# Weight sums on another engine, gate and sums in PSUM, and other PSUM banks for the early parts, in a one-layer encoder kernel on one core

## The chip, the cores and the metric

The kernel runs on one core of a Trainium2 chip. The metric is the device time of one execution in microseconds (us); the median of three runs stands for a kernel. The engines of the core are TensorE (PE in the profile; PEld is its weight load), VectorE (DVE), ScalarE (ACT), GpSimd (POOL) and SyncE (SP), which starts the DMA transfers.

## The reference

One layer of a streaming encoder on a sequence of 1024 tokens of 1024 features, in float32:

```
x = LN1(alpha*x + 0.5*SwiGLU_1(x))                      # FFN 1, width 2816
x = LN2(alpha*x + W_o[ RMS(FoX(x)) || RMS(ShortConv(x)) ])  # mixer
x = LN3(alpha*x + 0.5*SwiGLU_2(x))                      # FFN 2, width 2816
x = LN4(alpha*x + sigmoid(x W_g + b_g) * (p[i] W_p))      # gated embedding

def _swiglu(x, w_in, w_out):
    gu = x @ w_in
    gate, up = jnp.split(gu, 2, axis=-1)
    return (jax.nn.silu(gate) * up) @ w_out
```

FoX is causal attention with 8 heads of 64 and a forget gate; ShortConv is a gated causal convolution of width 3 over 512 channels. Both read one input projection.

## The kernel before, in words

**Products.** Every float32 operand is split into a high part (a cast by ScalarE) and a low part (source minus high part, by VectorE); `put` does this (line 122, its subtraction is line 124). `mm3` (140) then makes three matmuls of 128x512 (lines 142 to 144): high by high, high by low, low by high. The two large matrix products of each FFN and the mixer's input products go by a scheme with seven block products in place of eight (that of Strassen and Winograd), which needs sums of blocks of the activations (S1 to S4) and of the weights.

**Input products.** `turn0` (173) splits the blocks A11 and A12 of the activations. `turn1` (178) makes, for each of four slices k, the sums S3, S1, S2, S4 and the copy A22, and splits them. Its sums run through `tt` (135, operation at 137): a11 and a12 on GpSimd, s3, s1, s2 and s4 on VectorE, into SBUF tiles. In FFN 1 the blocks come from DRAM (`get_dram`, 198), elsewhere from r, the tokens by features, by TensorE transposes and a ScalarE pass (`get_ln`, 203). So that TensorE has work while the sums are made, the two of the seven products that need A11 and A12 alone run first for some column blocks: "early parts" (`ahead`, 279, with `part1`, 245, which evacuates the second product by VectorE at line 250). FFN 1 and FFN 2 have 10 early parts (`ffn_in`, 300; one step of `turn1` from the second part on in FFN 1), the mixer has 8 (loop at line 630; a step of `turn1` behind parts 4 to 7). All products take their bank from the one pool of eight PSUM banks. The rest runs in `pair` (284) and `part2` (260, evacuations at 262), with weight sums on GpSimd (`combos`, 253).

**Output products.** `ffn_out` (380) runs the seven products n = 0 to 6 one after the other. A product has 11 steps j of 12 matmuls; in each, a block H of the hidden activations and a block w of weights are split. The weight blocks come from functions `w_b11` to `w_b22` (406 to 430); `w_t3`, `w_t2` (417), `w_t4` and `w_t1` make 11 sums each on GpSimd, so 44 in each FFN. After a product, VectorE adds half of its four banks to r (line 467). r begins as the residual: `rest` (513) loads a quarter of x after another, and a multiplication follows, by ScalarE in FFN 1 (`init1`, line 523) and by GpSimd in FFN 2 (`init2`, line 976); this is spread over the products n = 0 to 3. In n = 5 and 6 the tokens are normalised (`norm`, 215; the power at 223 on GpSimd).

**Gate.** After FFN 2, `affine` (1051) applies the gain and offset of the third norm to r on GpSimd (lines 1055, 1056), rows 0 to 3 as soon as they are normalised. The product with W_g needs eight weight blocks (`w_block`) in each half. `gate` (1023) adds the bias on VectorE (1028) into an SBUF tile, takes the sigmoid on ScalarE (1029), multiplies by the embedding on GpSimd (1030) and adds to r on VectorE (1031). `finish_out` (1038) makes the last norm, four operations of VectorE for each row tile (1047, 1048), and stores.

The order of each engine's instructions is set by a scheduler that simulates the program, except where the code asks for program order. Each engine runs its list in order, and a DMA queue too.

Of the kernel before, what the change touches and what calls it, by code (L numbers as in the profile page):

```python
# [25 lines left out]
H = 8  # L26
# [25 lines left out]
def kernel(ctx: ExitStack, tc: tile.TileContext, x, xT, pT, f1_in, f1_out, f2_in,  # L52
# [60 lines left out]

    def load(src):
# [63 lines left out]
    def turn1(get, new=temp):  # L178
# [36 lines left out]
    def norm(r):  # L215
        st = small.tile([P, 2, 6], F32, name="st", tag="st")
        for i in range(2):
            nc.vector.bn_stats(st[:, i, :], r[:, half(i)])
        mv = small.tile([P, 2], F32, name="mv", tag="mv")
        nc.vector.bn_aggr(mv, st)  # L220
        rs = small.tile([P, 1], F32, name="rs", tag="rs")
        nc.vector.tensor_scalar(rs, mv[:, 1:2], LN_EPS, None, op0=add)
        nc.gpsimd.tensor_tensor(rs, rs, mhalf[:, 0:1], op=ALU.pow)
        nc.vector.tensor_scalar(r, r, mv[:, 0:1], rs, op0=sub, op1=mult)

# [74 lines left out]
    def ffn_in(w_in, get, early, wait, free, first=None):  # L300
# [60 lines left out]
        t1 = turn1(get, lambda: silp.tile([P, HB], F32, name="tt", tag="sil"))  # L361
# [6 lines left out]
        drain(t1)  # L368
        free()
# [8 lines left out]
        up.release()  # L378

    def ffn_out(w_out, init, after0, after1, extra=None):  # L380
# [24 lines left out]

        def w_b11(j):
# [12 lines left out]

        def w_t4(j):  # L420
            return tt(nc.gpsimd, load(w_out[j + NP][:, half(0)]), ztile(NP + j), sub)

        def w_t1(j):
            return tt(nc.gpsimd, load(w_out[j][:, half(1)]), ztile(j), sub)
# [14 lines left out]
        for n, (_, get_w, b, (i, nn)) in enumerate(prods):  # L439
# [21 lines left out]
            for t in range(4):  # L461
                for j, h, w in late:
                    mm3(ps[t], (h[0][:, tok(t)], h[1][:, tok(t)]), w, False, j == NP - 1, onto)
                if extra is not None and n in (0, 4):
                    mm(ps[t], ones_k, extra[n // 4], start=False, stop=True, skip_group_check=True)
                rs = r[4 * i + t][:, half(nn)]
                nc.vector.scalar_tensor_tensor(rs, ps[t], 0.5, rs, op0=mult, op1=add)
                if n == 6:
                    norm(r[4 + t])
# [159 lines left out]
    t1 = turn1(get_ln(r, 0), lambda: up.tile([P, HB], F32, name="tt", tag="u"))  # L629
    for i in range(8):  # L630
# [340 lines left out]
    def init2(r):  # L971
# [3 lines left out]
        for o, n in rest(r, z_d[1]):  # L975
            tc.keep_in_program_order(nc.gpsimd.tensor_tensor(o, o, gains[n], op=mult))
            yield

    def row_pair(o, n):


        a = [temp() for _ in range(n + 1)]
        for i, t in enumerate(a):
            nc.vector.memset(t[0:33], 0.0)
            for q in (0, 32):
                nc.sync.dma_start(t[q:q + 1], rows[3:4, half(i)])
        if n:
            nc.vector.tensor_tensor(a[1][0:33], a[1][0:33], a[0][0:33], op=sub)
        t, l = a[n], temp()
        nc.vector.tensor_scalar(t[0:33], t[0:33], 2 * ALPHA, None, op0=mult)  # L990
# [5 lines left out]
    def after0(r):  # L996
# [6 lines left out]
                        [row_pair(extra[n], n) for n in range(2)])  # L1003
# [19 lines left out]
    def gate(hf, t, ps, c0, w=HB, eng=nc.gpsimd):  # L1023
# [14 lines left out]
    def finish_out(t):  # L1038
# [5 lines left out]
        stt = nc.vector.scalar_tensor_tensor  # L1044
# [37 lines left out]
    for n in (1, 0):  # L1082
        for t in range(4):
            for q in range(2 if (n, t) == (0, 3) else 1):
# [5 lines left out]
                gate(1, t, ps, n * HB + q * w, w, nc.vector if w < HB else nc.gpsimd)  # L1090
# [3 lines left out]
    for t in outs:  # L1094
        finish_out(t)
# [72 lines left out]
```

## Time and profile before

| | before |
|---|---|
| runs, us | 1951.53, 1953.48, 1954.69 |
| median, us | 1953.48 |
| the profiled execution, us | 1955.81 |
| its span in the profile, us | 1954.0 |
| TensorE busy, us | 1874.5 |
| VectorE busy, us | 1442.4 |
| GpSimd busy, us | 997.6 |
| ScalarE busy, us | 799.8 |

The span runs from the first to the last instruction of the profile; 1.8 us lie outside it. The stages follow each other: input products of FFN 1 to about 445 us, its output products to 659, the mixer's input to 915, attention to 1140, the mixer's output to 1180, the input products of FFN 2 to 1596, its output products to 1844, then the gate. Busy shares of an engine do not say who waits for whom; a stretch is read by the matmuls in it, the granted clock (PEclk, 1.00 is 2.4 GHz) and what ended TensorE's waits.

### The profile page before, as it was taken

The page shows a single profiled execution, that of the slowest core. Times are in us where ns is not written, and L with a number is a line of the kernel's source. Part 1 is how long each engine was busy: PE and PEld are TensorE (multiplying, and loading weights), DVE is VectorE, ACT ScalarE, POOL GpSimd, SP SyncE. Part 2 cuts the span into 40 slices and gives each one's busy share as a digit, 9 for nine tenths or more (in the row PEclk, how much of TensorE's full clock was granted, in tenths as well). Part 3 has the DMA queues.
Part 4 walks back from the last instruction along what each step waited for, and adds up shares of the span by engine and source line. Part 5 has one row for each costly group of instructions (what it writes and reads, how often), then busy time and mean ns, then how long its engine had stood idle before and what let it go on. Part 6 is the DMA issues. An engine that isn't in the chain of part 4 may idle for free.

```text
span 1954.0 us, 25776 instructions
## 1 busy us (share of the span) xinstructions
PE 1874.5 (96%) x8632; PEld 1540.8 (79%) x8632; DVE 1442.4 (74%) x1999; ACT 799.8 (41%) x1420; POOL 997.6 (51%) x725
## 2 busy tenths in 40 slices
PE   8799999999999989999899999999999999899896
PEld 7688888888788868887688778888888887688685
DVE  7966555548767689976988877976555568987968
ACT  5322333325444553444665526433333334344430
POOL 2787566545550154431841322697565546850673
PEclk9899999999999999999999999999999999999998
DMA  7454323239555533378963123455332249554312
GB/s 238 150 185 163 117 102 119 96 121 379 171 186 178 183 115 119 105 253 273 267 172 91 56 91 118 146 194 178 105 124 93 97 139 365 186 189 152 123 59 98
DMA packets 167938, 307.60 MB, mean 157 GB/s; under 512 B 18503, under 2 KB 26951, under 8 KB 167805
## 3 DMA queue, kind: packets, MB, share of 16 engines
q1 hardware_dynamic: 167804, 305.95, 46.4%
q8 instruction: 68, 1.11, 0.2%
q14 instruction: 66, 0.53, 0.1%
HBM read 221.93 MB, written 83.95 MB: 157 GB/s over the span
## 4 chain that ended last, share of the span: by engine, by line
PE 76%; DVE 12%; issue 5%; DMA 3%; POOL 2%; ACT 1%; SPq 0%; DVEq 0%; ACTq 0%; POOLq 0%
PE ps L143 23%; PE ps L144 22%; PE ps L142 22%; DVE wl L124 4%; DVE tt L137 1%; PE pt L830 1%; PE pt L142 1%; PE pt L143 1%; PE pt L144 1%; PE ps_s L785 1%; PE po L838 1%; PE ps_s L782 1%; DVE S L124 1%; DVE pr L792 1%; PE po L837 1%
## 5 line engine op out<-in xcount | busy, mean ns | idle before, releaser
L142 PE MATMUL ps<-S,wh 128*128 128x512 f32 x896 | 350.8, 392 | 14.0 <-ACT S L123 6.5
L143 PE MATMUL ps<-S,wh 128*128 128x512 f32 x896 | 350.8, 392 | 4.0 <-DVE S L124 4.0
L144 PE MATMUL ps<-S,wl 128*128 128x512 f32 x896 | 350.2, 391 | 0.4 <-DVE wl L124 0.4
L123 ACT CAST wh<-tmp 128x512 fp32r<-128x512 f32 x268 | 164.7, 621 | 355.7 <-PE ps L143 268.5
L124 DVE TENSOR_TENSOR wl<-tmp,wh 128x512 fp32r<-128x512 f32 x268 | 256.8, 959 | 32.4 <-ACT wh L123 32.2
L143 PE MATMUL ps<-wl,wh 128*128 128x512 f32 x616 | 243.3, 395 | 15.1 <-DVE wl L124 15.1
L124 DVE TENSOR_TENSOR wl<-raw,wh 128x512 fp32r<-128x512 f32 x231 | 200.1, 870 | 75.7 <-ACT wh L123 75.4
L123 ACT CAST wh<-raw 128x512 fp32r<-128x512 f32 x239 | 146.6, 621 | 261.7 <-PE ps L143 208.3
L137 POOL TENSOR_TENSOR tmp<-raw 128x512 f32<-128x512 f32 x112 | 159.9, 1428 | 165.2 <-DVE wl L124 106.0
L144 PE MATMUL ps<-wh,wl 128*128 128x512 f32 x616 | 241.1, 391 | 0.0
L142 PE MATMUL ps<-wh 128*128 128x512 f32 x616 | 226.4, 393 | 0.7 <-ACT wh L123 0.7
L137 POOL TENSOR_TENSOR tmp<-raw,tmp 128x512 f32<-128x512 f32 x112 | 158.0, 1411 | 114.4 <-DVE wl L124 54.3
L142 PEld LDWEIGHTS ps<-S,wh 128*128 128x128 f32 x896 | 169.1, 189 | 50.5 <-ACT S L123 7.3
L143 PEld LDWEIGHTS ps<-S,wh 128*128 128x128 f32 x896 | 169.2, 189 | 40.5 <-DVE S L124 5.7
L144 PEld LDWEIGHTS ps<-S,wl 128*128 128x128 f32 x896 | 169.2, 189 | 36.2 <-DVE wl L124 1.1
L343 POOL TENSOR_TENSOR c<-c,sil 128x512 f32<-128x512 f32 x78 | 124.0, 1591 | 74.2 <-DVE c L250 43.3
L143 PEld LDWEIGHTS ps<-wl,wh 128*128 128x128 f32 x616 | 116.2, 189 | 45.8 <-DVE wl L124 22.2
L124 DVE TENSOR_TENSOR wl<-H,wh 128x512 fp32r<-128x512 f32 x154 | 147.4, 957 | 2.3 <-ACT wh L123 2.2
L142 PEld LDWEIGHTS ps<-wh 128*128 128x128 f32 x616 | 115.5, 188 | 25.8 <-ACT wh L123 1.8
L144 PEld LDWEIGHTS ps<-wh,wl 128*128 128x128 f32 x616 | 116.3, 189 | 23.5
L137 POOL TENSOR_TENSOR c<-c 128x512 f32<-128x512 f32 x88 | 128.1, 1460 | 6.7 <-DMA c<-e_d 1.9
L262 DVE TENSOR_TENSOR u<-ps,u 128x512 f32<-128x512 f32 x136 | 92.0, 683 | 47.2 <-PE ps L144 47.1
(299 smaller groups left out, 3988.0 us busy)
## 6 DMA issues: line engine op xcount, KB each, us to landing
raw<-in_f_in SPq DMA_DIRECT2D x216, 256.0 KB
h_d<-c SPq DMA_DIRECT2D x154, 256.0 KB
H<-h_d SPq DMA_DIRECT2D x154, 256.0 KB
raw<-in_f_out SPq DMA_DIRECT2D x132, 256.0 KB
z_d<-r SPq DMA_DIRECT2D x16, 512.0 KB
raw<-in_w_conv_in SPq DMA_DIRECT2D x32, 256.0 KB
r<-z_d SPq DMA_DIRECT2D x32, 256.0 KB
s_d<-s SPq DMA_DIRECT2D x28, 256.0 KB
```

The source lines that it names most:

```text
L123: nc.scalar.copy(h, src)
L124: (eng or nc.vector).tensor_tensor(l, src, h.bitcast(F32), op=sub)
L137: eng.tensor_tensor(t, a, b, op=op)
L142: mm(ps, a[0], b[0], start=first, stop=False, skip_group_check=onto)
L143: mm(ps, a[0], b[1], start=False, stop=False, skip_group_check=onto)
L144: mm(ps, a[1], b[0], start=False, stop=last, skip_group_check=onto)
L262: nc.vector.tensor_tensor(o, ps, u, op=add)
L343: nc.gpsimd.tensor_tensor(c, c, sil.pop((j, i, hf)), op=mult)
L782: mm(st[:, b:b + n], q["QA"][:, tok(t)], q["KA"][:, b:b + n], start=True, stop=False)
L785: mm(st[:, b:b + n], q["QB"][:, tok(t)], q["KB"][:, b:b + n], start=False, stop=True)
L792: nc.vector.tensor_scalar(pr[:, 0:w], pr[:, 0:w], l, None, op0=mult)
L830: nc.tensor.transpose(pv[:, j, t, :], prs[t][:, tok(2 * jp + j)], ident)
```

## The change

The four weight sums of each output step go from GpSimd to VectorE (`w_t3`, `w_t2`, `w_t4`, `w_t1`), three of them held back until a certain split of the product before (`sums`). The first product's evacuation goes to ScalarE as a scaled copy, and the residual is loaded and added during products 1 to 4. In `turn1` VectorE's sums are written to PSUM tiles of a pool of their own (three banks, while the early products have five), in FFN 2 and the mixer the A22 source too; in the mixer a step of `turn1` comes behind parts 1 to 4. In the gate the bias is added by a matmul, and sigmoid, product and sum read PSUM; the last norm's scale and shift go to ScalarE, its gain to VectorE and its offset to GpSimd (VectorE for the last row). GpSimd's `affine(0)` starts after the last of the eight powers.

```diff
+    def banks_anew(*n):
+        for q in reversed(psb):
+            q.release()
+        psb[:] = [pool(f"psb{i}", m, space=PSUM) for i, m in enumerate(n)]
...
-            s3 = tt(nc.vector, a11, a21, sub, new)
+            s3 = tt(nc.vector, a11, a21, sub, tbank)
...
-            a22 = get(1, k + 4, new)
+            a22 = get(1, k + 4, got or new)
...
-            s1 = tt(nc.vector, a21, a22, add, new)
+            s1 = tt(nc.vector, a21, a22, add, tbank)
...
-            s2 = tt(nc.vector, s1, a11, sub, new)
+            s2 = tt(nc.vector, s1, a11, sub, tbank)
...
-            s4 = tt(nc.vector, a12, s2, sub, new)
+            s4 = tt(nc.vector, a12, s2, sub, tbank)
...
-        t1 = turn1(get, lambda: silp.tile([P, HB], F32, name="tt", tag="sil"))
+        banks_anew(5, 3)
+        t1 = turn1(get, lambda: silp.tile([P, HB], F32, name="tt", tag="sil"),
+                   None if get is get_dram else tbank)
...
         drain(t1)
+        banks_anew(8)
...
+        def sums(n, j, o, a, b, op):
+
+            with tc.issue_after(done[n - 1, min(j + 5, NP - 1)]):
+                nc.vector.tensor_tensor(o, a, b, op=op)
+            return o
...
-            return tt(nc.gpsimd, b22, b12, sub, lambda: ztile(NP + j))
+            return tt(nc.vector, b22, b12, sub, lambda: ztile(NP + j))
...
-            tc.keep_in_program_order(nc.gpsimd.tensor_tensor(t, t, ztile(j), op=add))
-            return t
+            return sums(2, j, t, t, ztile(j), add)
...
-            return tt(nc.gpsimd, load(w_out[j + NP][:, half(0)]), ztile(NP + j), sub)
+            return sums(3, j, temp(), load(w_out[j + NP][:, half(0)]), ztile(NP + j), sub)
...
-                if n < 4 and j in (1, 3, 5, 7):
+                if n > 0 and n < 5 and j in (1, 3, 5, 7):
                     next(late_init)
...
-                nc.vector.scalar_tensor_tensor(rs, ps[t], 0.5, rs, op0=mult, op1=add)
+                if n == 0:
+                    nc.scalar.activation(rs, ps[t], AF.Copy, scale=0.5)
+                else:
+                    nc.vector.scalar_tensor_tensor(rs, ps[t], 0.5, rs, op0=mult, op1=add)
...
-        for i, nn in ((1, 0), (0, 1), (0, 0), (1, 1)):
+        for i, nn in ((0, 1), (0, 0), (1, 1), (1, 0)):
...
-        for o, _ in rest(r, x):
-            nc.scalar.mul(o, o, ALPHA)
+        for z, o, _ in rest(r, x):
+            if z is o:
+                nc.scalar.mul(o, o, ALPHA)
+            else:
+                nc.vector.scalar_tensor_tensor(o, z, ALPHA, o, op0=mult, op1=add)
...
-        if i > 3:
+        if 0 < i < 0 + 5:
             next(t1)
+    banks_anew(8)
...
-        pl, c = load(ple_d[tok(row), cs]), temp((P, w))
-        nc.vector.tensor_tensor(c, ps, bg[:, cs], op=add)
-        nc.scalar.activation(c, c, AF.Sigmoid)
-        eng.tensor_tensor(c, c, pl, op=mult)
-        nc.vector.tensor_tensor(r[row][:, cs], r[row][:, cs], c, op=add)
+        pl = load(ple_d[tok(row), cs])
+        mm(ps, ones_k, bg[c0 // HB][:, c0 % HB:c0 % HB + w], start=False, stop=True,
+           skip_group_check=True)
+        nc.scalar.activation(ps, ps, AF.Sigmoid)
+        nc.vector.tensor_tensor(ps, ps, pl, op=mult)
+        nc.vector.tensor_tensor(r[row][:, cs], ps, r[row][:, cs], op=add)
...
-            stt(o, o, mv[:, 0:1], gb4[n], op0=sub, op1=mult)
-            stt(o, o, rs, gb4[2 + n], op0=mult, op1=add)
+            nc.scalar.activation(o, o, AF.Identity, bias=off, scale=rs)
+            nc.vector.tensor_tensor(o, o, gb4[n], op=mult)
+            eng.tensor_tensor(o, o, gb4[2 + n], op=add)
...
-    affine(0)
+    with tc.issue_after(last_norm[0]):
+        affine(0)
```

Three places in the order of the instructions show what moves; the line numbers of the changed kernel differ (`put` is line 132 there, `tt` 145, the evacuation of `part1` 261, the held sums 427, the evacuation of `ffn_out` 494, the power of `norm` 233, `affine` 1096).

VectorE in the mixer's early parts, before: u is the evacuation of the fifth part, tt are the sums, and S3, A22, S1, S2 the low halves.

```order
L250 TENSOR_TENSOR u_6323<-ps_6310,s1_6304 128x512
L124 TENSOR_TENSOR wl_6655<-tmp_6647,wh_6654 128x512
L579 SCALAR_TENSOR_TENSOR spl_6326<-u_6323,sph_6325 128x512
L137 TENSOR_TENSOR tt_6341<-tt_6339,tt_6337 128x512
L137 TENSOR_TENSOR tt_6354<-tt_6337,tt_6350 128x512
L124 TENSOR_TENSOR wl_6674<-tmp_6649,wh_6673 128x512
L137 TENSOR_TENSOR tt_6358<-tt_6354,tt_6339 128x512
L124 TENSOR_TENSOR S3_6078<-tt_6341,S3_6076 128x512
L124 TENSOR_TENSOR A22_6086<-tt_6350,A22_6084 128x512
L124 TENSOR_TENSOR S1_6082<-tt_6354,S1_6080 128x512
L124 TENSOR_TENSOR S2_6074<-tt_6358,S2_6072 128x512
```

The same sums in the changed kernel: cc are the evacuations of the second and the third part, pt the sums in PSUM.

```order
L261 TENSOR_TENSOR cc_6217<-ps_6204,s1_6198 128x512
L132 TENSOR_TENSOR wl_6504<-raw_6499,wh_6503 128x512
L145 TENSOR_TENSOR pt_6229<-tt_6227,tt_6225 128x512
L132 TENSOR_TENSOR wl_6523<-raw_6501,wh_6522 128x512
L132 TENSOR_TENSOR S3_6094<-pt_6229,S3_6092 128x512
L132 TENSOR_TENSOR A22_6102<-pt_6238,A22_6100 128x512
L145 TENSOR_TENSOR pt_6242<-tt_6225,pt_6238 128x512
L261 TENSOR_TENSOR cc_6296<-ps_6283,s1_6277 128x512
L132 TENSOR_TENSOR wl_6553<-raw_6548,wh_6552 128x512
L132 TENSOR_TENSOR S1_6098<-pt_6242,S1_6096 128x512
L145 TENSOR_TENSOR pt_6246<-pt_6242,tt_6227 128x512
L132 TENSOR_TENSOR S2_6090<-pt_6246,S2_6088 128x512
```

The first sums moved from behind the fifth part to behind the second, and each low half now has a PSUM source.

VectorE in the output products of FFN 1, before, at the end of a product (r is an evacuation).

```order
L124 TENSOR_TENSOR wl<-T,wh 128x512
L124 TENSOR_TENSOR wl<-H,wh 128x512
L124 TENSOR_TENSOR wl<-tmp,wh 128x512
L124 TENSOR_TENSOR wl<-H,wh 128x512
L124 TENSOR_TENSOR wl<-tmp,wh 128x512
L467 SCALAR_TENSOR_TENSOR r_3959<-ps,r_3959 128x512
L124 TENSOR_TENSOR wl<-H,wh 128x512
```

The changed kernel, in the middle of the product n = 2, whose steps carry the sums of the next (tmp<-raw,T).

```order
L132 TENSOR_TENSOR wl<-T,wh 128x512
L427 TENSOR_TENSOR tmp<-raw,T 128x512
L132 TENSOR_TENSOR wl<-H,wh 128x512
L132 TENSOR_TENSOR wl<-T,wh 128x512
L427 TENSOR_TENSOR tmp<-raw,T 128x512
L132 TENSOR_TENSOR wl<-H,wh 128x512
L132 TENSOR_TENSOR wl<-T,wh 128x512
L427 TENSOR_TENSOR tmp<-raw,T 128x512
```

Two low halves a step became two low halves and a sum.

GpSimd at the end of the output products of FFN 2, before: rs are powers, r0 to r3 the affine steps.

```order
L1056 TENSOR_TENSOR r0_15489<-r0_15489,gb3_17608 128x512
L1056 TENSOR_TENSOR r1_15490<-r1_15490,gb3_17608 128x512
L1056 TENSOR_TENSOR r2_15491<-r2_15491,gb3_17608 128x512
L1056 TENSOR_TENSOR r3_15492<-r3_15492,gb3_17608 128x512
L223 TENSOR_TENSOR rs_17544<-rs_17544,mhalf_100 128x1
L223 TENSOR_TENSOR rs_17563<-rs_17563,mhalf_100 128x1
```

The changed kernel at the same place.

```order
L233 TENSOR_TENSOR rs_17592<-rs_17592,mhalf_100 128x1
L233 TENSOR_TENSOR rs_17611<-rs_17611,mhalf_100 128x1
L233 TENSOR_TENSOR rs_17630<-rs_17630,mhalf_100 128x1
L233 TENSOR_TENSOR rs_17649<-rs_17649,mhalf_100 128x1
L1096 TENSOR_TENSOR r0_15529<-r0_15529,gb3_17656 128x512
L1096 TENSOR_TENSOR r1_15530<-r1_15530,gb3_17656 128x512
```

All sixteen affine operations of rows 0 to 3 moved behind the powers of rows 4 to 7.

## Rows read from the trace of the kernel before

**Rows 1.** The page's busy time by engine, whole span.

```profile
PE 1874.5 (96%) x8632; PEld 1540.8 (79%) x8632; DVE 1442.4 (74%) x1999; ACT 799.8 (41%) x1420; POOL 997.6 (51%) x725
```

**Rows 2.** Stretches of the span; x counts instructions, the line's head names the columns.

```profile
core 0: us, PE busy (x) PEld busy (x) DVE busy (x) ACT busy (x) POOL busy (x), PEclk, DMA share, GB/s
60.00:84.00 24.00, 13.07 (x48) 9.69 (x47) 23.92 (x26) 10.68 (x20) 15.18 (x10) 0.79 0.41 142
504.00:516.00 12.00, 10.43 (x43) 7.45 (x42) 9.93 (x14) 5.54 (x11) 8.20 (x6) 1.00 0.76 248
...
704.00:724.00 20.00, 12.88 (x48) 9.61 (x47) 20.00 (x25) 10.15 (x18) 9.42 (x7) 0.83 0.26 92
1300.00:1400.00 100.00, 100.00 (x443) 82.84 (x442) 63.16 (x81) 31.21 (x51) 76.96 (x54) 1.00 0.47 162
...
1656.00:1700.00 44.00, 38.69 (x158) 28.57 (x157) 44.00 (x32) 14.84 (x26) 41.96 (x26) 1.00 0.62 209
...
1824.00:1844.00 20.00, 11.16 (x43) 8.11 (x42) 20.00 (x15) 8.13 (x14) 17.61 (x11) 0.83 0.36 120
1936.00:1954.00 18.00, 0.03 (x1) 0.00 (x0) 14.36 (x30) 1.46 (x3) 4.14 (x4) 0.56 0.24 88
```

**Rows 3.** TensorE's waits from 58 to 84 us: total, times, longest.

```profile
PE ps L142 <- ACT S L123: 6.5, 1, 6.5
PE ps L143 <- DVE S L124: 2.6, 1, 2.6
PE ps L142 <- DVE sil L250: 1.8, 1, 1.8
```

**Rows 4.** TensorE's waits from 1822 to 1846 us.

```profile
PE ps L143 <- DVE wl L124: 8.8, 2, 7.8
```

**Rows 5.** VectorE's groups, whole span: busy, mean ns, idle before and its releaser.

```profile
L262 DVE TENSOR_TENSOR u<-ps,u 128x512 f32<-128x512 f32 x136 | 92.0, 683 | 47.2 <-PE ps L144 47.1
...
L124 DVE TENSOR_TENSOR pt<-pt 128x512 fp32r<-128x512 f32 x80 | 53.4, 681 | 7.5 <-ACT pt L123 7.0
```

**Rows 6.** VectorE's timeline from 1658 us: start, duration, instruction.

```profile
1658.28 1.78 DVE L124 TENSOR_TENSOR wl<-T,wh 128x512 fp32r<-128x512 f32 x1
1659.98 0.68 DVE L124 TENSOR_TENSOR wl<-H,wh 128x512 fp32r<-128x512 f32 x1
1660.58 1.78 DVE L124 TENSOR_TENSOR wl<-T,wh 128x512 fp32r<-128x512 f32 x1
```

**Rows 7.** VectorE's groups from 34 to 79 us.

```profile
L137 DVE TENSOR_TENSOR tt<-tt 128x512 f32<-128x512 f32 x13 | 16.4, 1263 | 0.7 <-DMA tt<-in_xT 0.7
L124 DVE TENSOR_TENSOR S<-tt,S 128x512 fp32r<-128x512 f32 x14 | 14.5, 1044 | 0.1
L124 DVE TENSOR_TENSOR wl<-raw,wh 128x512 fp32r<-128x512 f32 x7 | 8.5, 1219 | 0.0
```

**Rows 8.** ScalarE's timeline at 509 us.

```profile
509.03 0.63 ACT L523 ACTIVATE r<-r 128x512 f32<-128x512 f32 x1 [6.56 <-DMA r<-in_x]
```

**Rows 9.** GpSimd's groups, whole span.

```profile
L137 POOL TENSOR_TENSOR T<-raw 128x512 f32<-128x512 f32 x22 | 31.8, 1457 | 41.5 <-DMA raw<-in_f_out 32.4 <-PE ps L143 9.0
L976 POOL TENSOR_TENSOR r<-r,gains 128x512 f32<-128x512 f32 x16 | 26.2, 1660 | 3.0 <-ACT gb L494 3.0
```

**Rows 10.** GpSimd's line 1055: shortest, median, longest in ns; first and last start.

```profile
L1055 POOL TENSOR_TENSOR r<-r,gb x16: 1287/1710/1756, 1815.0 to 1891.1; 128x512 f32<-128x512 f32 x16
```

**Rows 11.** TensorE's line 465, the same columns.

```profile
L465 PE MATMUL ps<-extra,ones_k x8: 388/399/499, 1638.9 to 1769.2; 33*128 33x512 f32 x8
```

**Rows 12.** VectorE's groups from 1936 us to the end.

```profile
L1048 DVE SCALAR_TENSOR_TENSOR r<-r,rs,gb 128x512 f32<-128x512 f32 x6 | 5.2, 912 | 0.0
L1047 DVE SCALAR_TENSOR_TENSOR r<-r,mv,gb 128x512 f32<-128x512 f32 x6 | 4.2, 744 | 0.0
...
L1028 DVE TENSOR_TENSOR tmp<-ps,bg 128x256 f32<-128x256 f32 (+1 forms) x3 | 1.5, 489 | 0.0
```

**Rows 13.** Timelines of VectorE, GpSimd and ScalarE in the tail.

```profile
1949.08 1.41 DVE L1048 SCALAR_TENSOR_TENSOR r<-r,rs,gb 128x512 f32<-128x512 f32 x2
...
1947.99 0.92 POOL L1043 TENSOR_TENSOR rs<-rs,mhalf 128x1 f32<-128x1 f32 x1 [3.34 <-DVE rs L1042]
...
1936.94 0.63 ACT L1029 ACTIVATE tmp<-tmp 128x512 f32<-128x512 f32 x1 [4.10 <-DVE rs L1042]
```

More of the change, by code (lines that the diff above doesn't have):

```diff
@@ L222, in norm @@
         nc.vector.tensor_scalar(rs, mv[:, 1:2], LN_EPS, None, op0=add)
-        nc.gpsimd.tensor_tensor(rs, rs, mhalf[:, 0:1], op=ALU.pow)
+        power = nc.gpsimd.tensor_tensor(rs, rs, mhalf[:, 0:1], op=ALU.pow)
         nc.vector.tensor_scalar(r, r, mv[:, 0:1], rs, op0=sub, op1=mult)
+        return power.ins
     later = []
@@ L412, in w_t3 @@
             b22, b12 = load(w_out[j + NP][:, half(1)]), load(w_out[j][:, half(1)])
-            return tt(nc.gpsimd, b22, b12, sub, lambda: ztile(NP + j))
+            return tt(nc.vector, b22, b12, sub, lambda: ztile(NP + j))
         def w_t2(j):
             t = ztile(NP + j)
-            tc.keep_in_program_order(nc.gpsimd.tensor_tensor(t, t, ztile(j), op=add))
-            return t
+            return sums(2, j, t, t, ztile(j), add)
         def w_t4(j):
-            return tt(nc.gpsimd, load(w_out[j + NP][:, half(0)]), ztile(NP + j), sub)
+            return sums(3, j, temp(), load(w_out[j + NP][:, half(0)]), ztile(NP + j), sub)
         def w_t1(j):
-            return tt(nc.gpsimd, load(w_out[j][:, half(1)]), ztile(j), sub)
+            return sums(4, j, temp(), load(w_out[j][:, half(1)]), ztile(j), sub)
         def w_b21(j):
@@ L466, in ffn_out @@
                 rs = r[4 * i + t][:, half(nn)]
-                nc.vector.scalar_tensor_tensor(rs, ps[t], 0.5, rs, op0=mult, op1=add)
+                if n == 0:
+                    nc.scalar.activation(rs, ps[t], AF.Copy, scale=0.5)
+                else:
+                    nc.vector.scalar_tensor_tensor(rs, ps[t], 0.5, rs, op0=mult, op1=add)
                 if n == 6:
-                    norm(r[4 + t])
+                    last_norm[0] = norm(r[4 + t])
             if n == 5:
@@ L513, in rest @@
     def rest(r, src):
-        for i, nn in ((1, 0), (0, 1), (0, 0), (1, 1)):
+        for i, nn in ((0, 1), (0, 0), (1, 1), (1, 0)):
             for t in range(4 * i, 4 * i + 4):
                 o = r[t][:, half(nn)]
-                tc.keep_in_program_order(nc.sync.dma_start(o, src[tok(t), half(nn)]))
-                yield o, nn
+                z = temp() if (i, nn) == (1, 0) else o
+                tc.keep_in_program_order(nc.sync.dma_start(z, src[tok(t), half(nn)]))
+                yield z, o, nn
     def init1(r):
-        for o, _ in rest(r, x):
-            nc.scalar.mul(o, o, ALPHA)
+        for z, o, _ in rest(r, x):
[3 more added lines that the diff above has]
+                nc.vector.scalar_tensor_tensor(o, z, ALPHA, o, op0=mult, op1=add)
             yield
@@ L974, in init2, with row_pair @@
             nc.scalar.mul(gains[n], gains[n], ALPHA)
-        for o, n in rest(r, z_d[1]):
-            tc.keep_in_program_order(nc.gpsimd.tensor_tensor(o, o, gains[n], op=mult))
+        for z, o, n in rest(r, z_d[1]):
+            tc.keep_in_program_order(nc.gpsimd.tensor_tensor(z, z, gains[n], op=mult))
+            if z is not o:
+                tc.keep_in_program_order(nc.gpsimd.tensor_tensor(o, o, z, op=add))
             yield
-    def row_pair(o, n):
-        a = [temp() for _ in range(n + 1)]
+    def row_pair(o, row, n, scale, step):
+        a = [temp() for _ in range(2 if step else 1)]
         for i, t in enumerate(a):
@@ L985, in row_pair @@
             for q in (0, 32):
[L986 to L990, printed above, removed]
+                nc.sync.dma_start(t[q:q + 1], rows[row:row + 1, half(n - i)])
+        t, l = a[0], temp()
+        if step:
+            nc.vector.tensor_tensor(t[0:33], t[0:33], a[1][0:33], op=sub)
+        if scale != 1.0:
+            nc.vector.tensor_scalar(t[0:33], t[0:33], scale, None, op0=mult)
         nc.scalar.copy(o[0:33], t[0:33])
@@ L1002 @@
     r, rA, rB = ffn_out(f2_out, init2, after0, lambda r: None,
-                        [row_pair(extra[n], n) for n in range(2)])
+                        [row_pair(extra[n], 3, n, 2 * ALPHA, n == 1) for n in range(2)])
     gp = pool("gp")
@@ L1070 @@
                 X["A22"] = slots((2, 3), "A22h"), slots((14, 15), "A22l")
-                bg = slot(16, "bg", F32, (P, D))
-                nc.sync.dma_start(bg, rows[8].partition_broadcast(P))
+                bg = [row_pair(o, 8, i, 1.0, False) for i, o in enumerate(slots((16,), "bg"))]
             if n == 0 and k >= 4 or n == 1 and k < 4:
@@ L1089 @@
                     mm3(ps, x_blk(1, k, t), b, k == 0, k == KT - 1)
-                gate(1, t, ps, n * HB + q * w, w, nc.vector if w < HB else nc.gpsimd)
+                gate(1, t, ps, n * HB + q * w, w)
             outs.append(t if n else 4 + t)
```

23 lines of the change are left out of this document (15 added, 8 removed).

## The prediction

> **What bounds the kernel now.** I read the page's busy table first: TensorE is busy for 1874.5 us, 96% of the span, VectorE for 1442.4 [rows 1]. So what can be won is small, and it lies where TensorE does not run at its usual rate. I therefore cut the span into stretches and read TensorE's matmuls in each. An undisturbed stretch has 443 matmuls in 100 us, 0.2257 us each [rows 2]; what a stretch lost is its length less its matmuls times that, which takes in idle time and the low clock behind it. The stretches of the places that the diff touches [rows 2] give: A, 60 to 84: 24 - 48 x 0.2257 = 13.2 us lost; B, 504 to 516: 2.3; C, 704 to 724: 9.2; H, 1656 to 1700: 8.3; I, 1824 to 1844: 10.3. After the last matmul, at 1936, come 18 us of tail. Together that is 61 us. In A, C, H and I VectorE is busy without a gap (23.92 of 24, 20 of 20, 44 of 44, 20 of 20), and the granted clock falls to 0.79 in A and 0.83 in C and I. What TensorE waits for there is VectorE, or a copy behind its queue: in A one wait of 6.5 us for ScalarE's half of an S block, 2.6 us for VectorE's half and 1.8 us for an evacuation [rows 3], in I 8.8 us for a wl [rows 4].
>
> Why VectorE is late is shown by the durations. With one input in PSUM its 128x512 operations take 0.68 us on average over the whole span, 136 and 80 of them [rows 5]. With both inputs in SBUF they take 0.68 us or 1.78 us: in H three neighbours start at 1658.28, 1659.98 and 1660.58, so a slow one holds the queue for 1.70 us and a quick one for 0.60 [rows 6]. GpSimd is busy for 41.96 of the 44 us of H and for 17.61 of 20 in I [rows 2]. I read this as VectorE waiting for GpSimd when both read SBUF, which an input in PSUM avoids; a slow one costs 1.10 us more. The Trainium skill ("SBUF — State Buffer", Who interferes with whom) says the same: two SBUF inputs on VectorE contend with a GpSimd instruction that reads SBUF, under an exclusive lock, and one does not.
>
> **The change, part by part.** All terms are differences of the end, in us.
>
> *A, the first sums.* From 34 to 79 VectorE did 13 sums at 1263 ns, 14 S halves at 1044 and 7 wl at 1219 [rows 7]. With the sums in PSUM, all S halves and half of the sums (s2 and s4) have a PSUM input: 14 x (1.044 - 0.68) + 6.5 x (1.263 - 0.68) = 5.1 + 3.8 = 8.9. VectorE's queue is full there, so the last S2 half comes about that much earlier, against 10.9 us of waits [rows 3]. In this FFN s3 and s1 still have two SBUF inputs, as has each wl. I take -8; the ends are -4 (GpSimd's reads find the other operations instead) and -12.5.
>
> *Five banks.* The early products have 5 PSUM banks where they had 8. A product lasts 12 x 0.2257 = 2.7 us, so TensorE can be 13.5 us ahead of the evacuations and no more 21.7. The evacuations come earlier in VectorE's order, which covers it; without that cover it comes back as a stall in A or C. I count it with the hiccups below.
>
> *B, the late additions.* ScalarE multiplied the residual into r during products 0 to 3, and once waited 6.56 us for x to land while casts of wh stood behind it [rows 8]. Now product 0 is written to r by ScalarE with a scale, four copies that replace four VectorE operations, and the loads come from product 1 on. The same wait can come back later. -1.5, between -2.3 and 0.
>
> *C, the mixer's sums.* They stood behind the fifth to eighth early part, with the S2 product right after; now they stand behind the second to fifth, and three parts of two products, 6 x 2.7 = 16.3 us of TensorE work, lie between. That exceeds the 9.2 lost, so the stall should go. What is late next is the norm of row 7, which the transposes now want sooner; some of this may show. -8, between -7 and -9.2.
>
> *H, the weight sums.* 44 sums in each output stage go from GpSimd to VectorE. For each step of 12 matmuls (2.71 us) VectorE then has three operations, 3 x 0.60 = 1.80, and with 4 evacuations in 11 steps 2.02. So it keeps up, if the operations are quick; with two slow ones among three it would not (4.2). GpSimd keeps only the 16 gains, at 1660 ns, and 4 added sums [rows 9]; 20 x 1.10 = 22 us spread over some 44 steps is 0.5 a step, 2.5 against 2.71. That is tight. -6 of the 8.3; the ends are -8.3 and -3. In the first output stage GpSimd has nothing left beside the powers, and nothing was lost there but B.
>
> *I, the last norm.* GpSimd's affine step on rows 0 to 3 began at 1815.0, during the last steps of the output product [rows 10]; it now starts after the last power. So VectorE's halves there take 0.60 us a piece: 15 operations in 20 us [rows 2] shrink to 9 or 10. Its 16 operations are then nearer to the first gate, whose addition on VectorE could wait for them a little. -9.5, between -7 and -10.3.
>
> *The gate.* 15 matmuls of 512 columns and two of 256 add the bias, with the same 33-row weight as those that took 399 ns like any other [rows 11], so 0.2257 each: +3.6 on TensorE, which sets the pace there. VectorE's additions of the bias and GpSimd's products leave; sigmoids now read and write PSUM on ScalarE, which the matmuls of that stage hide; if they did not, it would show in the tail only, where the chain below has it.
>
> *The tail.* VectorE works 14.36 of 18 us there, its order never waiting for long: twelve operations of the norm, 5.2 + 4.2 us, and three additions of the bias, 1.5 [rows 12]. The last one ends at 1950.49, and 3.5 us go to the store [rows 13]. After: six products (6 x 0.68 = 4.1) and two additions (1.4) replace the 10.9 us, so VectorE needs 14.4 - 10.9 + 5.5 = 9.0 us. A power takes 0.92, an operation of ScalarE 0.63 [rows 13]; VectorE's queue waits for some of that, an estimated 1 us. So 9 + 1 + 3.5 = 13.5. -4.5, between -7 and 0: nothing is won if GpSimd's two additions of the row before stand ahead of the last power.
>
> *Hiccups.* Transfers that GpSimd waited for are now waited for by VectorE, in order: +2, between 0 and +8 with the banks.
>
> Sum: -8 - 1.5 - 8 - 6 - 9.5 + 3.6 - 4.5 + 2 = -31.9. The profiled execution took 1955.8 us, which makes 1923.9. It stands 2.3 above the median of the runs, 1953.48, so a median run should take **1921.6 us**. All best ends give 1953.5 - 46.0 = 1907.5, all worst ends 1953.5 - 10.4 = 1943.
>
> **Rivals.** (1) *VectorE becomes the bound of the output stages.* GpSimd waited 32.4 us for raw weights before the sums T<-raw, at no cost, since it ran ahead [rows 9]. VectorE takes them in its order, with every wl behind. If it waited as long, TensorE would lose 32.4 us, and with the low clock that follows (10.3 lost for 8.8 of waits in I) 38: 1921.6 + 38 = 1960, slower. It decides from a loss of 32 us on. For it: the sums are in order among the wl. Against it: the order places them five or more steps (13.5 us) ahead of their use, and fewer transfers start in product 0.
>
> (2) *The collisions move rather than go.* The moved sums have two SBUF inputs and so meet the gains; s1, s3 and wl still meet GpSimd's sums in A. H stays whole, A is halved, and the hiccups are at their upper end: -4 - 1.5 - 8 - 9.5 + 3.6 - 4.5 + 8 = -15.9, 1937.6. For it: two inputs in SBUF, as in rows 6. Against it: GpSimd's own work in H shrinks from 41.96 us in 44 to 20 operations in four products. That same page of the Trainium skill, by its rule, speaks for this rival, as no moved sum has an input in PSUM.
>
> (3) *Five banks are too few.* Half of A and of C returns: +8, 1930. For it: VectorE is full in A. Against it: evacuations stand earlier.
>
> **How the numbers follow.** Forecast as worked out 0.70, rival (1) 0.08, rival (2) 0.12, rival (3) 0.08, and 0.02 for something else. The forecast's bounds, 1907.5 to 1943, take in (2) and (3); I leave out (1) and the rest, and some of the worst ends. A measurement here can tell about 0.2%, 4 us, from no change. Faster than that: nearly all of the forecast, (2) and (3), 0.87. Slower: (1) and a bit, 0.09. Same 0.04.
>
> **What would show it.** In the changed profile: TensorE's stretch behind the first sums should have some 80 matmuls in 24 us or lose under 6 us; the mixer's first S2 product should follow without a wait; wl in the second output stage should average near 0.75 us and not 1.67; the steps before the gate should run at full clock; the time from last matmul to end should be 13 to 14 us. I am wrong if VectorE's weight sums show waits for transfers with TensorE idle behind, or if the wl stay at 1.7 us.

## The result and the profile after

The changed kernel took 1928.25 us in the median of four runs (1922.86 to 1931.37), the one before 1954.09 in four; the ratio is 0.9861, with a 95% interval of 0.983 to 0.9892, so it is faster by 1.1 to 1.7%. The forecast was 1921.6 with a range of 1907.5 to 1943. The sum of the parts was near (-31.9 against -25.8 of the medians), but three of the parts were not (A, the mixer, the gate): errors of both signs cancelled, and that is luck. The profiled execution took 1931.37 us, its span is 1929.6.

To see where the time went, I cut both spans at the same matmuls. These lines of TensorE's timeline are the cuts in the changed kernel: the first and last matmul of FFN 1's output, the last large score matmul of attention, the first and last of FFN 2's output, and the last of all.

```profile
430.08 0.39 PE L151 MATMUL ps<-wl,wh 128*128 128x512 f32 x1
...
642.71 0.39 PE L151 MATMUL ps<-wl,wh 128*128 128x512 f32 x1
...
1108.12 0.40 PE L816 MATMUL ps_s<-KA,QA 128*128 128x512 f32 x1
...
1598.45 0.40 PE L151 MATMUL ps<-wl,wh 128*128 128x512 f32 x1
...
1818.90 0.39 PE L151 MATMUL ps<-wl,wh 128*128 128x512 f32 x1
...
1917.72 0.38 PE L1066 MATMUL ps<-bg,ones_k 33*128 33x256 f32 x1
```

The same cuts in the timeline of the kernel before:

```profile
442.21 0.39 PE L143 MATMUL ps<-wl,wh 128*128 128x512 f32 x1
...
657.35 0.39 PE L143 MATMUL ps<-wl,wh 128*128 128x512 f32 x1
...
1120.81 0.39 PE L782 MATMUL ps_s<-KA,QA 128*128 128x512 f32 x1
...
1609.37 0.39 PE L143 MATMUL ps<-wl,wh 128*128 128x512 f32 x1
...
1844.31 0.40 PE L143 MATMUL ps<-wl,wh 128*128 128x512 f32 x1
...
1935.75 0.28 PE L144 MATMUL ps<-wg,A22l 128*128 128x256 f32 x1
```

Their differences, with the terms of the forecast:

| stretch, us | before | after | difference | forecast |
|---|---|---|---|---|
| FFN 1 input | 442.2 | 430.1 | -12.1 | A -8 |
| FFN 1 output | 215.1 | 212.6 | -2.5 | B -1.5 |
| mixer input and attention | 463.5 | 465.4 | +1.9 | C -8 |
| mixer output and FFN 2 input | 488.6 | 490.3 | +1.7 | 0 |
| FFN 2 output | 234.9 | 220.5 | -14.4 | H and I -15.5 |
| gate | 91.4 | 98.8 | +7.4 | +3.6 |
| last matmul to end | 18.2 | 11.9 | -6.3 | -4.5 |
| sum | 1954.0 | 1929.6 | -24.4 | -31.9 with +2 for hiccups |

The distances of one stretch differ between kernels that share its code: 428.6 to 432.8 for FFN 1's input, 460.2 to 467.2 for the mixer and attention, 217.3 to 220.5 for FFN 2's output (the profiled execution above is the longest there). So a difference of some 3 us in these, or 7 in the mixer and attention, is not told from none; FFN 1's output agrees within 1 (212.6 to 213.4).

Stretches of [rows 2] after the change, each at its place in the changed kernel:

```profile
core 0: us, PE busy (x) PEld busy (x) DVE busy (x) ACT busy (x) POOL busy (x), PEclk, DMA share, GB/s
60.00:84.00 24.00, 24.00 (x108) 19.87 (x107) 21.68 (x28) 10.78 (x19) 15.56 (x13) 1.00 0.46 165
675.00:685.00 10.00, 7.42 (x33) 5.62 (x31) 9.95 (x15) 6.30 (x11) 8.55 (x7) 1.00 0.51 179
685.00:697.00 12.00, 9.76 (x44) 7.74 (x42) 11.83 (x18) 7.57 (x14) 5.95 (x5) 1.00 0.49 173
1632.00:1676.00 44.00, 44.00 (x195) 36.44 (x195) 40.41 (x52) 19.37 (x35) 17.46 (x10) 1.00 0.66 239
1800.00:1819.00 19.00, 19.00 (x95) 15.78 (x94) 16.36 (x26) 16.22 (x29) 0.00 (x0) 1.00 0.57 186
```

A, the first line, holds 108 matmuls where [rows 2] had 48, at full clock. H (1632 to 1676) holds 195 in 44 us, the rate of an undisturbed stretch (0.2256 us each), with GpSimd busy for 17.46 us and not 41.96. Before the gate GpSimd does nothing. Between 675 and 697, in the mixer, TensorE has only 77 matmuls in 22 us and VectorE is full: a stall is still there, in another place. TensorE's waits in the 73 us after FFN 1's output, first before (from 657 us), then with the change (from 642 us):

```profile
PE ps L142 <- ACT s L248: 5.7, 1, 5.7
PE ps L143 <- DVE S L124: 1.4, 2, 1.1
```

```profile
PE ps L150 <- ACT s L259: 4.0, 2, 2.4
PE ps L150 <- ACT S L131: 1.6, 1, 1.6
PE ps L150 <- DVE S L132: 1.2, 1, 1.2
```

One long wait ahead of the S products became several short ones.

VectorE's groups from 34 to 79 us, against [rows 7]:

```profile
L132 DVE TENSOR_TENSOR S<-pt,S 128x512 fp32r<-128x512 f32 x13 | 8.6, 682 | 0.0
L132 DVE TENSOR_TENSOR wl<-raw,wh 128x512 fp32r<-128x512 f32 x8 | 8.4, 1051 | 0.0
L145 DVE TENSOR_TENSOR pt<-tt 128x512 f32<-128x512 f32 x6 | 4.2, 694 | 0.0
```

The S halves fell from 1044 to 682 ns. The sums whose two inputs are still in SBUF (pt<-tt) were quick as well (694 ns). That is not because they write PSUM, since four of that kind take 1458 ns in a run below. Three of them did run beside an operation of GpSimd, and there it was GpSimd's that took longer: 2.52, 1.83 and 1.63 us, where its undisturbed ones take 1.30. The wl, which read SBUF twice, were slow (1051).

### The profile page after: what moved, and what is told of

Read it like the earlier page. It is cut to its first block, busy times and chain, and to the rows that moved or that the text cites. A ratio compares the mean times of both kernels' runs of the same rounds, so it can differ in the third digit from the quotient of the medians.

```text
span 1929.6 us, 25703 instructions
## 1 busy us (share of the span) xinstructions
PE 1876.5 (97%) x8649; PEld 1541.5 (80%) x8649; DVE 1381.3 (72%) x2079; ACT 817.1 (42%) x1444; POOL 849.7 (44%) x640
## 4 chain that ended last, share of the span: by engine, by line
PE 56%; DVE 4%; DMA 2%; ACT 1%; issue 1%; POOL 0%; POOLq 0%; DVEq 0%; ACTq 0%; SPq 0%
PE ps L150 16%; PE ps L151 16%; PE ps L152 16%; PE pt L864 1%; PE pt L150 1%; PE pt L152 1%; PE pt L151 1%; PE po L872 1%; DMA raw<-in_pT 1%; DVE wl L132 1%; PE po L871 1%; PE ps_s L819 1%; DVE pr L826 1%; DVE m L821 1%; PE ps_s L816 1%
## 5 line engine op out<-in xcount | busy, mean ns | idle before, releaser
L132 DVE TENSOR_TENSOR wl<-raw,wh 128x512 fp32r<-128x512 f32 x231 | 202.6, 880 | 71.7 <-ACT wh L131 71.2
L132 DVE TENSOR_TENSOR wl<-tmp,wh 128x512 fp32r<-128x512 f32 x268 | 235.1, 878 | 21.9 <-ACT wh L131 21.8
L150 PE MATMUL ps<-wh 128*128 128x512 f32 x616 | 220.3, 392 | 0.0
L233 POOL TENSOR_TENSOR rs<-rs,mhalf 128x1 f32<-128x1 f32 x24 | 18.6, 816 | 313.2 <-DVE rs L232 252.6
```

Source lines behind the costliest of these rows:

```text
L132: return (eng or nc.vector).tensor_tensor(l, src, h.bitcast(F32), op=sub)
L150: mm(ps, a[0], b[0], start=first, stop=False, skip_group_check=onto)
```

## The experiments

Most undo or add one part in the changed kernel; the later ones join several. Where no number of runs is given, the kernel ran once, and its distances are what counts. "Mixer" below is the distance from the last output matmul of FFN 1 to the mixer's last S matmul: 255.7 us before, 259.2 in the changed kernel.

**FFN 1's first sums back in SBUF, eight banks.**

```diff
-            s3 = tt(nc.vector, a11, a21, sub, tbank)
+            s3 = tt(nc.vector, a11, a21, sub, sbk)   # sbk: SBUF in FFN 1, tbank elsewhere
```

> The changed kernel with the first sums of FFN 1 back in SBUF and eight banks for its early products. Theory (two SBUF inputs collide with GpSimd): VectorE's S halves there take 1.0 us on average again in place of 0.68, TensorE loses 10 to 13 us between 60 and 84, and FFN 1's output products start at 440 to 443 in place of 430.1. Rival (the gain of 12 us in FFN 1 comes from the order, since the evacuations stand earlier, or from the banks): the start stays at 430 to 434.

It took 1936.1 us; FFN 1's input 443.9 in place of 430.1. VectorE's groups from 34 to 79 us, and the stretch A:

```profile
L145 DVE TENSOR_TENSOR tt<-tt 128x512 f32<-128x512 f32 x14 | 17.1, 1220 | 0.7 <-DMA tt<-in_xT 0.7
L132 DVE TENSOR_TENSOR S<-tt,S 128x512 fp32r<-128x512 f32 x14 | 13.4, 965 | 0.1
```

```profile
60.00:84.00 24.00, 13.39 (x39) 9.57 (x38) 23.92 (x27) 9.72 (x18) 15.17 (x10) 0.72 0.44 131
```

The whole of A goes with the sums in PSUM, and VectorE's halves and sums are slow again, as the theory says: the rival's 430 to 434 did not come. The run gives back the eight banks too, so the number of banks is not tried apart from the place of the sums.

**The weight sums back on GpSimd.**

```diff
-            return sums(3, j, temp(), load(w_out[j + NP][:, half(0)]), ztile(NP + j), sub)
+            return tt(nc.gpsimd, load(w_out[j + NP][:, half(0)]), ztile(NP + j), sub)
```

(and the other three likewise)

> The changed kernel with the 44 weight sums of each output stage back on GpSimd. Theory (GpSimd's reads hold up VectorE's halves): the wl<-H and wl<-T of the second output stage take 1.2 us or more on average, TensorE loses 6 to 9 us in its first half, and the stage, 218 to 220 us from the first to the last of its matmuls, takes 225 to 228; the first output stage stays at 212.7, within 2. Rival (the later start of the residual, products 1 to 4 with four fewer transfers at the crowded beginning, is what helped): the second stage stays within 2 us of 218 to 220.

1940.51 us. FFN 2's output took 224.5 us, 4 to 7 more than the 217.3 to 220.5 of the kernels with the sums on VectorE, and FFN 1's output 216.0 against 212.6. Whole-span groups, first of this run, then of the changed kernel:

```profile
L132 DVE TENSOR_TENSOR wl<-H,wh 128x512 fp32r<-128x512 f32 x154 | 148.4, 964 | 2.0 <-ACT wh L131 2.0
...
L132 DVE TENSOR_TENSOR wl<-T,wh 128x512 fp32r<-128x512 f32 x66 | 78.6, 1191 | 26.4 <-ACT wh L131 26.3
```

```profile
L132 DVE TENSOR_TENSOR wl<-H,wh 128x512 fp32r<-128x512 f32 x154 | 114.4, 743 | 2.3 <-ACT wh L131 2.3
...
L132 DVE TENSOR_TENSOR wl<-T,wh 128x512 fp32r<-128x512 f32 x66 | 53.9, 817 | 30.3 <-ACT wh L131 30.1
```

In the changed kernel VectorE has 44 more operations a stage, and the low halves alone gave back 34.0 + 24.7 us. In the second stage alone the wl<-H take 1062 ns here and 767 in the changed kernel, the wl<-T 1186 and 845: near the expected 1.2 us, but under it. The loss came in at the low end of the expectation in FFN 2, and from 1630 to 1700 us TensorE lost 70 - 288 x 0.2257 = 5.0 us in place of 6 to 9. FFN 1's stage lost more than the 2 us allowed. With the late additions but the sums on GpSimd it took 216.0, against 215.1 before the change: so the gain of 2.5 us there, which I had put down to the late additions, does not show without the sums on VectorE.

**The affine step issued early.**

```diff
-    with tc.issue_after(last_norm[0]):
-        affine(0)
+    affine(0)
```

> The changed kernel with GpSimd's affine step on rows 0 to 3 issued as soon as it can be. Theory: VectorE's halves in the last steps of the second output stage take 1.7 us again, TensorE waits for one of them for 7 to 9 us, and the stage takes 227 to 230 us in place of 218 to 220. Rival (the stall there came from GpSimd's weight sums further ahead having made VectorE late): the stage stays at 218 to 221.

1942.88 us; FFN 2's output took 228.5. VectorE's groups from 1800 to 1828 us, and TensorE's waits:

```profile
L132 DVE TENSOR_TENSOR wg<-raw,wg 128x512 fp32r<-128x512 f32 x7 | 12.0, 1764 | 0.0
L132 DVE TENSOR_TENSOR wl<-H,wh 128x512 fp32r<-128x512 f32 x3 | 5.3, 1773 | 0.0
```

```profile
PE ps L151 <- DVE wl L132: 7.8, 1, 7.8
```

The wait of 7.8 us is that of [rows 4] again, at the same size. This one line of the change is worth 8 to 11 us.

**The mixer's part: four kernels.** The first has the sums in SBUF, eight banks, and the steps behind parts 4 to 7, as before the change:

```diff
-        if 0 < i < 0 + 5:
+        if i > 3:
```

> The changed kernel with the mixer's part of the change undone: its first sums in SBUF, eight banks for its products, the steps behind parts 4 to 7. Measured by the profiles: from the last output matmul of FFN 1 to the first attention matmul 264.2 us before and 268.0 after. Theory 1 (the mixer's part costs time, since VectorE is the bound there, with its sums earlier and PSUM tiles of only three banks as a chain): that distance falls back to 264 to 265, and the time is 3 to 4 us under that of the changed kernel, some 1924.5. Theory 2 (the stall in the mixer comes from the stage before, whose last norm and weight halves crowd VectorE, and not from the mixer's part): the distance stays at 267 or more, and the time at 1928.

1926.12 us (four runs, 1925.07 to 1929.04): within the scatter of the changed kernel, and between the times of the two theories. Its mixer took 256.2, the mixer with attention 462.1. To the first attention matmul it took 269.6, so by the distance named in the expectation theory 2 holds; that distance moves with attention's own start, and I no longer lean on it. By the mixer's own distance the part costs 3 us, as theory 1 says, and this repeats: four kernels with the changed kernel's order of instructions up to the first S product take 258.7 to 259.2 (the changed one and those with the weight sums on GpSimd, the early affine step and the 128-row bias), three with the order of before take 255.7 to 256.2 (before, this one and the first attempt below). In the whole time it is lost in the scatter of attention.

Early steps with SBUF:

> The changed kernel with the mixer's first sums in SBUF and eight banks for its products, but the steps behind parts 1 to 4 as in the change. Theory 1a (the three banks of the sums and the five of the products hold the steps up): the wait ahead of the S products goes, at least 6 us, and the first S product starts at 691 or before in place of 697.2. Theory 1b (VectorE's whole work up to there is the bound, whatever the banks): the sums meet GpSimd's weight sums, some 8 of them for 1.1 us each, and the first S product starts at 700 to 708.

1924.32 us; the first S product at 700.6, the mixer 258.5: as theory 1b says, and theory 1a, which asked for 691, falls. Late steps with PSUM:

> The changed kernel with the mixer's steps moved back behind parts 4 to 7, the sums still in PSUM with five and three banks. Theory 1a (banks): still a wait, the first S product at 697 or later. Theory 1b (VectorE's work): the sums are quick there, as their inputs are in PSUM, and the wait that the kernel before has behind its last part (9.2 us lost) shrinks by some 5 us, so the first S product starts at 690 to 693.

1937.58 us; the mixer 270.4, the worst. The first S product came at 698.8: a wait of 8.0 us ahead of it, and 7.1 more for the S blocks after it. Theory 1b falls here, and 1a's 697 or later holds; neither alone fits both runs. Stretches of that run:

```profile
688.00:700.00 12.00, 4.02 (x20) 3.21 (x19) 11.62 (x19) 7.28 (x14) 6.45 (x5) 0.83 0.39 138
700.00:718.00 18.00, 10.18 (x22) 5.98 (x21) 10.84 (x17) 5.68 (x10) 2.82 (x3) 0.50 0.08 26
```

Until 700 VectorE is full; afterwards it idles 7 of 18 us, and its timeline has one S half each 1.94 us, each behind its cast:

```profile
701.24 0.69 DVE L132 TENSOR_TENSOR S<-pt,S 128x512 fp32r<-128x512 f32 x1 [0.65 <-ACT S L131]
703.18 0.69 DVE L132 TENSOR_TENSOR S<-pt,S 128x512 fp32r<-128x512 f32 x1 [0.65 <-ACT S L131]
```

So a step of sums has a length of its own in VectorE's order, sum, cast, half, next sum, which nothing covers when it stands last. That three banks and not the sums themselves make the chain was not tried apart.

Then I took work off VectorE: low halves of the early parts' weights on GpSimd, 16 or 8 of them, beside 128-row bias matmuls (below).

```diff
-        ps = product(split(b21), "A12")
+        ps = product(split(b21, eng=eng[1]), "A12")   # nc.gpsimd in the mixer's early parts
```

> The changed kernel with 128-row bias matmuls (gate and output products), and in the mixer's eight early parts all 16 low halves of the weights subtracted by GpSimd in place of VectorE. Theory 1 (VectorE's whole work between the last output product of FFN 1 and the S blocks is the bound of the mixer's beginning): 16 x 0.6 to 0.9 us leave VectorE, and from the last output matmul of FFN 1 to the last S matmul of the mixer it takes 249 to 253 us in place of 256 to 259. Theory 2 (the chain of sums through three PSUM banks, and VectorE and ScalarE waiting for each other in their fixed orders, is the bound): it stays at 256 to 260. Theory 3 (GpSimd, with 1.3 us or more each and its own sums in the same queue, delivers too late): over 260.

> As the run with 16 low halves on GpSimd, but only the second of each part, eight of them. Theory 1: half the effect, 252 to 256 us. Theory 2: 256 to 260. Theory 3: under 256 here while the run with 16 is over 260.

With 16 the mixer took 258.5 (1926.39 us, two runs), with 8 it took 255.7 (1917.81, two runs). In the first, VectorE waited for GpSimd (groups from 640 to 700 us):

```profile
L145 DVE TENSOR_TENSOR pt<-tt 128x512 f32<-128x512 f32 x4 | 5.8, 1458 | 3.1 <-POOL tt L145 3.1
L234 DVE TENSOR_SCALAR r<-r,mv,rs 128x1024 f32<-128x1024 f32 x4 | 5.0, 1295 | 4.6 <-POOL rs L233 4.6
```

Eight is the half effect that theory 1 asks for; the run with 16 lies in theory 2's 256 to 260. But the one with FFN 1's sums in SBUF has the change's own mixer and takes 255.0 too. The scheduler gave that kernel another order of VectorE's instructions there, and TensorE and ScalarE the same order as in the kernel with eight. So these 3 us are not shown to come from the work moved; an order of instructions gives them back without it.

**The bias as 128 rows.**

```diff
-    ones_k = const.tile([33, P], F32R, name="ones_k")
+    ones_k = const.tile([P, P], F32R, name="ones_k")
...
-                bg = [row_pair(o, 8, i, 1.0, False) for i, o in enumerate(slots((16,), "bg"))]
+                bg = [row_pair(o, 8, i, 1.0, False, P) for i, o in enumerate(slots((16,), "bg"))]
```

> The changed kernel with the bias of the gate as a 128-row weight and operand (the rows 33 to 127 of the bias hold zeros), nothing else. In the changed kernel the 17 bias matmuls have 33 rows; one alone among the others has 0.32 us before, 0.42 to 0.43 behind and 0.33 after that to the next start, 1.08 in place of 0.45 without it; four in a row take 1.78. Theory 1 (the change of the row count is what costs: the weights of such a matmul are loaded only when it starts): with 128 rows each costs 0.2257 us, the gate stage shortens by 3.5 to 4 us, the time is near 1924.5. Theory 2 (a matmul of another weight into the bank costs that by itself, by the bank's handover to ScalarE): the distances stay as they are, and the time at 1928.

1924.57 us (four runs), 0.9842 of before (0.9822 to 0.9862). TensorE's timeline around one bias matmul, first in the changed kernel, then here:

```profile
1898.41 0.39 PE L152 MATMUL ps<-wg,A22l 128*128 128x512 f32 x1
1898.73 0.50 PE L1066 MATMUL ps<-bg,ones_k 33*128 33x512 f32 x1
1899.16 0.50 PE L150 MATMUL ps<-wg,A21h 128*128 128x512 f32 x1
1899.49 0.39 PE L151 MATMUL ps<-wg,A21h 128*128 128x512 f32 x1
```

```profile
1898.52 0.40 PE L152 MATMUL ps<-wg,A22l 128*128 128x512 f32 x1
1898.76 0.40 PE L1066 MATMUL ps<-bg,ones_k 128*128 128x512 f32 x1
1898.99 0.39 PE L150 MATMUL ps<-wg,A21h 128*128 128x512 f32 x1
1899.22 0.39 PE L151 MATMUL ps<-wg,A21h 128*128 128x512 f32 x1
```

The three steps between starts sum to 1.08 us in the first and 0.70 in the second. From the first bias matmul to the first of the last two it is 71.7 us in the changed kernel (1842.67 to 1914.35) and 68.3 here, 3.4 less, near the 3.5 of theory 1. The row count was the price, not the handover. The whole gate stage shortened only from 98.8 to 96.8, since up to the first bias matmul it took 1.7 us longer here; in the four later kernels with 128 rows it takes 94.9 to 96.3.

**The first attempt at a better one.** It joins 128 rows for the bias and for the eight row additions of the output products, the mixer undone, and row 6's offsets on VectorE:

```diff
-                finish_out(outs.pop(0))
+                o = outs.pop(0)
+                finish_out(o, nc.vector if o == 6 else nc.gpsimd)
```

> The changed kernel with four edits: the bias of the gate and the two rows added to the output products as 128-row matmuls; the offsets of row 6 in the last norm on VectorE, as for row 7; and the mixer's part undone (sums in SBUF, eight banks, steps behind parts 4 to 7). Expected from the terms: 3.4 us for the bias, 0.9 for the eight other rows (four in a row take 1.78 with 33 rows), 2 to 3 for the tail (the last power waits for GpSimd's two additions of row 6, 2.97 us), 2 for the mixer: 1928.25 - 8.8 = 1919.5, between 1916 and 1923. A rival for the tail: VectorE's two more operations delay the chain of row 7 by as much as the wait for GpSimd, and from the last matmul to the end it stays at 11.2 to 12.1 us; else 9 to 10.

1920.02 us (four runs). The total is as expected, the tail is not: last matmul to end 12.8 us, the rival's side. VectorE's timeline there:

```profile
1913.28 0.68 DVE L1086 TENSOR_TENSOR r<-r,gb 128x512 f32<-128x512 f32 x1
1913.88 0.42 DVE L1066 TENSOR_TENSOR ps<-ps,raw 128x256 f32<-128x256 f32 x1
1914.21 0.68 DVE L1086 TENSOR_TENSOR r<-r,gb 128x512 f32<-128x512 f32 x1
```

The two offsets (L1086) stand around row 7's last product, and the 1.2 us they take outweigh the wait for GpSimd (at most 0.56 us in the changed kernel).

**The last pair, five rounds each**, both with 128 rows throughout, without the tail edit:

> The same kernel as the run with eight low halves on GpSimd, timed again in five rounds: the changed kernel with 128-row bias matmuls in gate and output products and eight of the early parts' 16 low halves on GpSimd in the mixer. From two runs 1917.8; expected 1916 to 1922, that is 6 to 12 us under the changed kernel and 1.7 to 2.0% under the one before.

> The same, but with the mixer's sums undone (SBUF, eight banks, steps behind parts 4 to 7) and eight low halves on GpSimd. If the mixer's beginning is bound by VectorE's work over the whole stretch, the place of the sums does not matter: within 2 us of the other. If GpSimd's eight operations meet the late sums, which have two SBUF inputs here, VectorE's S halves take over 1 us, and it is 3 to 8 us slower.

1920.11 us (ratio 0.9821, 0.9802 to 0.9839) and 1920.9 (the same ratio and interval). The place and kind of the mixer's sums decide nothing that can be measured in the time here. In the profiles the second pays in S halves of 1.10 us on average, and its mixer takes 259.0 against 255.9. The first is 8 us under the changed kernel in the median, though their intervals overlap a little.

## Why the prediction came out as it did

**A** was the mechanism as told, undersized: -12.1, near the end of -12.5. The term that was too small is "half of the sums (s2 and s4) have a PSUM input": s1 and s3 were counted as still slow and took 694 ns. With all 13 sums quick the working gives 14 x 0.36 + 13 x 0.58 = 12.7.

**B** came out at -2.5 against -1.5, but not by the cause given: with the sums on GpSimd and the additions late, nothing of it is left (216.0). The prediction said that "nothing was lost there but B" in that stage, yet its wl<-H fell from 879 to 721 ns.

**C** is the step that was wrong: "that exceeds the 9.2 lost, so the stall should go". I looked at TensorE's cover behind the sums and not at what VectorE has to do ahead of them. Moved forward, the sums meet the norms, the evacuations and 16 low halves; VectorE, 9.95 of 10 and 11.83 of 12 us busy, is late again: the first S2 product still waits, and the mixer takes 3.5 us longer than before (259.2 against 255.7). The stretch of the mixer and attention changed by +1.9, within its scatter. Whether VectorE's sum of work, the order of its list or the chain of a step sets it is not settled: the run with late steps in PSUM shows the chain, the one with FFN 1's sums in SBUF that the same mixer code in another order takes 4.2 us less, and the ones with low halves moved leave the sum of work open. Rival (3), too few banks, took nothing from A; in the mixer it stays open.

**H and I**: -14.4 against -15.5, and each undone costs what it was given: 4 to 7 us for H, forecast 6, and 8 to 11 us for I, forecast 9.5. Rival (1), VectorE waiting for weights, did not show: the 66 held sums of both stages idle the engine only behind GpSimd's late additions, for 3.7 us, and the 22 that are not held wait 1.7 us for transfers.

```profile
L427 DVE TENSOR_TENSOR tmp<-raw,T 128x512 f32<-128x512 f32 x44 | 32.0, 735 | 3.8 <-POOL r L1012 3.7
L145 DVE TENSOR_TENSOR T<-raw 128x512 f32<-128x512 f32 x22 | 17.5, 807 | 2.2 <-DMA raw<-in_f_out 1.7 <-PE ps L151 0.4
```

Rival (2) did a little: wl<-T at 817 ns, not 680. Over the second output stage all wl took 0.77 us on average, as forecast; before it was 1.08, and the 1.67 of the forecast's signs holds in stretch H alone.

**The gate** is the second step that failed: "399 ns like any other [rows 11], so 0.2257 each". The duration of a pipelined matmul is not its price. The distance between starts is, and alone among others a 33-row one costs 1.08 - 0.45 = 0.63 us, four in a row (1.78 - 0.45) / 4 = 0.33; +7.4 in place of +3.6. Seven alone and twice four in a row, of 512 columns, make about 7 of it. The starts around line 465 in the trace before would have shown the second of these.

**The tail**: -6.3 against -4.5. GpSimd's two additions did stand ahead of the last power, the case for which the prediction saw nothing won, but they cost 0.56 us at most: its input was ready at 1921.05 and it started at 1921.61.

```profile
1918.68 2.97 POOL L1089 TENSOR_TENSOR r<-r,gb 128x512 f32<-128x512 f32 x2 [1.85 <-DVE r L1088]
1921.61 0.54 POOL L1082 TENSOR_TENSOR rs<-rs,mhalf 128x1 f32<-128x1 f32 x1
```

VectorE's last operation ended 8.1 us after the last matmul, where the working had 9 + 1.

**FFN 2's input** was given no term and lost 1.7; its distance is 488.6 before and 489.6 to 490.4 with the change in all runs, and no run took it apart.

**The range**: the worst ends sum to -9.4, not -10.4, so its upper end should have been 1944. It decides nothing.

## What to carry to other kernels

Count what an engine must do before a step that is moved forward, not only what covers it behind: an earlier place in the list of a full VectorE gave nothing back in the mixer. Where GpSimd and VectorE both read SBUF, look first for an input of VectorE that can be in PSUM, or a step of GpSimd that can start later: these were worth 12 and 8 to 11 us here, moving 44 sums from GpSimd to VectorE 4 to 7 in one stage and 3.4 in the other. Price a matmul by the distance between starts, and pad a lone one with few rows to the row count of its neighbours.

## What the runs showed of the hardware

A matmul of 33 rows among matmuls of 128 costs 0.63 us where one of 128 rows costs 0.25 (1.08 and 0.70 us less 0.45), and its weight load starts with it, not ahead (both at 1898.73; with 128 rows 1898.53 and 1898.76):

```profile
1898.73 0.18 PEld L1066 LDWEIGHTS ps<-bg,ones_k 33*128 33x128 f32 x1 [0.35 <-issue]
```

```profile
1898.53 0.19 PEld L1066 LDWEIGHTS ps<-bg,ones_k 128*128 128x128 f32 x1
```

Operations of VectorE with one tensor input were slow beside GpSimd too: the scaling of r by TENSOR_SCALAR (128x1024), at 804 ns on average before, took 1295 in the run with 16 low halves on GpSimd (four from 640 to 700 us: two of 0.81 us, and two of 1.78 beside GpSimd's halves).
